# Two float32 blocks on one core: the order on the engines taken from the scheduler's detailed timeline

## The chip, the core and the metric

One core of one Trainium2 chip. The metric is the device time of one execution in microseconds (us). Engines: PE (TensorE), DVE (VectorE), ACT (ScalarE), POOL (GpSimd), SP (SyncE, which issues the loads).

## What is computed

A batch of one, 512 tokens, 1024 features, all in float32. Block 1 is an attention with compressed, selected and windowed keys beside a depthwise convolution of 31 taps, each branch with a merge gate, and then a feed-forward with a convolution of 3 taps. Block 2 has two layers whose norms are modulated by a vector `c`.

```
x = x + (g_a * y_attn + g_b * y_conv) @ w_out            # g_a, g_b: sigmoid of two parts of h @ w_in
x = x + conv_ffn(rms_norm(x, norm2_g), w_up, dw, dw_b, w_down)
return rms_norm(x, final_g)                              # end of block 1
...
mod = silu(c) @ ada_w[layer] + ada_b[layer]              # block 2: shift, scale, gate
h = rms_norm_2(x, norm_w[layer]) * (1.0 + scale) + shift
x = x + gate * mixer(h)                                  # layer 0: dense and latent attention; layer 1: a window with sinks
```

## The kernel before

Features lie on the 128 partitions and the 512 tokens along them, so x is eight tiles of 128x512. A float32 product is made of three matmuls: a weight is split into a high and a low part (`wload`: load L108 by SP, high part L109 by ACT, low part L110 by POOL, for some weights by DVE), the activations likewise, and `mm3` issues low x high (L123), high x low (L124) and high x high (L125). A gemm with 1024 inputs is thus 24 matmuls into one PSUM bank. There are two `pg` and two `ps` banks (the wide gemms go through all four), three `pt` banks for transposes and one `po` bank for attention outputs. A gemm can't begin before the bank that it takes has been read out.

The stages, by the time at which they ran in the profiled execution:
- 0 to 94 us, projections. The first norm's row R1 comes from `Squares` (L209, L216), `rsqrt` (L156 to L170) and a broadcast by PE (L176). The windows for compressed keys are copied by ACT in eight pieces each (L326). The four value gemms of 280 columns (`pg125_516`, `pg128_548`, ...) are read out by ACT (L394). Key stacks are made by ACT (L233, L235) and DVE; the weights of the compression are split at L338.
- 94 to 345 us, attention of block 1, merge gates and the depthwise convolution. Of a half-head (one branch of one head; there are 16) PE makes four score tiles (L501), DVE takes the bias and the maximum (L505), ACT the exponential (L507), DVE a reciprocal (L508), POOL the scaling (L509); PE transposes (L253), ACT and DVE copy it out as two parts (L257, L258), PE multiplies by the values (L263), and L524 adds the compressed branch. DVE's L270 closes a head. The 31 taps over four tiles are 120 DVE instructions at L586 (tap 0 is ACT's). The merge gates are gemms that DVE reads out at L575. Behind the last tap come the layer norm's sums (L601, L602) and L605.
- 345 to 437 us, branch projections and `w_o`. From 437 us the second norm: L170, the chain L156 to L165 on DVE, the broadcast L176 on PE, and R2 copied by DVE at L182.
- 437 to 612 us, up projections of the feed-forward. For every up gemm DVE reads out the bank (L666, it needs R2), ACT starts the convolution (L668), and DVE adds two taps (L670). In between, DVE makes the modulation of block 2: 96 multiply-and-sum instructions at L652 on rows loaded at L651, and 48 small ones at L654.
- 612 to 870 us, down projections; the last one goes by halves of the tokens (`by_halves`: L740 reads a bank out and adds, L722 and L724 make the normed input).
- 870 to 1182 us, layer 0 of block 2 (scores L869, transposes L854, gates as gemms), and 1182 to 1387 us, layer 1.

The order on each engine isn't written by hand. `build` records the instructions in the order of its code; when the `TileContext` closes, its scheduler decides from their dependencies, and from estimates of how long each takes, in which order every engine issues its own. Five places (`with after()`, L247) hold a piece back behind a named instruction. The order is fixed once the program is made: an engine works in that order, and an instruction that waits holds up all that is behind it on its engine.

```
549            with after():
550                conv_start(0)
...
583            for c in range(4):
584                V.scalar_tensor_tensor(conv[c], zs[c][:, t:t + 512], ...)
...
        u = new("p", (128, 514))
        V.tensor_mul(u[:, 2:514], ps, R2)                # L666
```

## Time and profile before

| | |
|---|---|
| median of 3 runs | 1388.19 us (1386.32 to 1389.37) |
| the profiled execution, its span | 1387.6 us |
| busy in the span: PE, DVE, ACT, POOL | 1284.6, 983.8, 690.1, 707.2 us |
[...]

The profiled execution is shown by its span, from the first instruction to the end of the last; it lies 0.6 us under the median. Of PE's 103 us without a matmul some 18 lie in the first 94 us, 24 in the attention of block 1, 21 in the up projections and the norm ahead of them, 9 in the halves around 840 us. In the other stages PE is busy for 95% and more, or the idle time is at the end.

### The profile page before, as it was taken

To read this page: it belongs to the slowest core of one execution; us is meant where nothing else is said; L and a number is where in the kernel's file an instruction comes from. 1 tells how busy PE (TensorE), PEld (TensorE's weight loads), DVE (VectorE), ACT (ScalarE), POOL (GpSimd) and SP (SyncE) were. 2 spreads that over 40 slices of the span, in tenths; PEclk is the share of its full clock that TensorE was granted. 3 is DMA by queue.
4 is the path that set the end of the run, shared out by engine and by line. 5 is a ranking of instruction groups with operands and counts; after the bars stand their busy time and mean duration, and the time that the engine had idled before them with its cause. 6 is when DMAs were issued, how large, how long until landed. Compare 5 with 4: busy or idle time off the path is not lost.

```text
span 1387.6 us, 19249 instructions
## 1 busy us (share of the span) xinstructions
PE 1284.6 (93%) x6337; PEld 1052.3 (76%) x6337; DVE 983.8 (71%) x2117; ACT 690.1 (50%) x1467; POOL 707.2 (51%) x669
## 2 busy tenths in 40 slices
PE   6888889989999998889999997899999989999997
PEld 5777778767877876668888887777777778788886
DVE  7559999984545999972266548967688876666455
ACT  6735467325343323333344434367676745777554
POOL 4248475453643545466555526625444631676642
PEclk9999899999999998999999998999999999999998
DMA  7121101322344777724332320211111120212221
GB/s 222 46 84 56 37 31 56 114 78 82 107 122 129 234 226 228 229 85 137 99 92 78 109 80 26 77 39 35 50 62 39 39 62 28 64 54 62 61 77 61
DMA packets 71971, 124.74 MB, mean 90 GB/s; under 512 B 8256, under 2 KB 17344, under 8 KB 71872
## 3 DMA queue, kind: packets, MB, share of 16 engines
q1 hardware_dynamic: 71872, 123.52, 29.3%
q8 instruction: 50, 0.82, 0.3%
q14 instruction: 49, 0.40, 0.1%
HBM read 121.39 MB, written 2.10 MB: 89 GB/s over the span
## 4 chain that ended last, share of the span: by engine, by line
PE 59%; DVE 28%; ACT 5%; issue 4%; POOL 2%; DMA 2%; SPq 0%; DVEq 0%; ACTq 0%; POOLq 0%
PE pg L123 11%; PE pg L125 10%; PE pg L124 10%; DVE h L586 6%; PE po L263 5%; PE ps L123 4%; PE ps L124 4%; PE ps L125 4%; PE pt L253 3%; DVE p L670 3%; DVE b L652 2%; PE ps L869 2%; DVE z L652 2%; PE ps L1054 2%; PE ps L501 1%
## 5 line engine op out<-in xcount | busy, mean ns | idle before, releaser
L110 POOL TENSOR_TENSOR wl<-wr,wh 128x512 fp32r<-128x512 f32 (+2 forms) x215 | 296.7, 1383 | 319.2 <-ACT wh L109 256.9
L123 PE MATMUL pg<-h,wl 128*128 128x512 f32 x692 | 281.3, 407 | 8.5 <-DVE m L575 5.1
L124 PE MATMUL pg<-h,wh 128*128 128x512 f32 x692 | 277.3, 401 | 0.0
L125 PE MATMUL pg<-h,wh 128*128 128x512 f32 x692 | 276.5, 400 | 0.0
L109 ACT ACTIVATE wh<-wr 128x512 fp32r<-128x512 f32 (+2 forms) x215 | 131.7, 617 | 133.5 <-PE pg L125 74.5
L123 PEld LDWEIGHTS pg<-h,wl 128*128 128x128 f32 x692 | 131.6, 190 | 39.2 <-issue 11.6
L125 PEld LDWEIGHTS pg<-h,wh 128*128 128x128 f32 x692 | 131.6, 190 | 28.3
L124 PEld LDWEIGHTS pg<-h,wh 128*128 128x128 f32 x692 | 131.6, 190 | 27.3 <-issue 0.7
L110 POOL TENSOR_TENSOR m<-t,m 128x512 fp32r<-128x512 f32 (+1 forms) x67 | 93.3, 1392 | 78.7 <-ACT m L109 50.5
L670 DVE SCALAR_TENSOR_TENSOR p<-p,k,p 128x512 f32<-128x512 f32 x88 | 100.4, 1141 | 26.3 <-ACT p L668 25.4
L263 PE MATMUL po<-t,h 128*128 128x512 f32 (+3 forms) x384 | 111.5, 367 | 5.3 <-DVE t L258 2.7
L258 DVE TENSOR_TENSOR t<-pt,t 128x512 fp32r<-128x512 f32 (+1 forms) x160 | 97.3, 629 | 24.9 <-ACT t L257 24.3
L586 DVE SCALAR_TENSOR_TENSOR h<-z,k,h 128x512 f32<-128x512 f32 x120 | 113.4, 988 | 0.1
L257 ACT ACTIVATE t<-pt 128x512 fp32r<-128x512 f32 (+1 forms) x160 | 84.1, 551 | 26.3 <-PE pt L253 25.6
L253 PE MATMUL pt<-k,p 128*128 128x128 f32 x576 | 88.8, 276 | 1.7 <-POOL p L509 0.8
L263 PEld LDWEIGHTS po<-t,h 128*128 128x128 f32 x384 | 67.5, 192 | 27.2 <-ACT t L257 12.0
L253 PEld LDWEIGHTS pt<-k,p 128*128 128x128 f32 x576 | 70.1, 141 | 15.6 <-POOL p L876 3.5
L123 PE MATMUL ps<-h,wl 128*128 128x512 f32 x196 | 78.5, 401 | 1.8 <-ACT h L147 1.6
L124 PE MATMUL ps<-h,wh 128*128 128x512 f32 x196 | 78.0, 398 | 0.3 <-DVE h L148 0.2
L125 PE MATMUL ps<-h,wh 128*128 128x512 f32 x196 | 77.9, 397 | 0.0
L876 POOL TENSOR_SCALAR p<-p,s 128x512 f32<-128x512 f32 x64 | 44.9, 705 | 63.0 <-DVE s L875 62.4
L123 PE MATMUL ps<-h,m 128*128 128x512 f32 (+1 forms) x148 | 59.6, 402 | 15.5 <-DVE p L666 15.4
(367 smaller groups left out, 3003.5 us busy)
## 6 DMA issues: line engine op xcount, KB each, us to landing
b<-ada_t SPq DMA_DIRECT2D x48, 256.0 KB, 3.4
z<-ada_t SPq DMA_DIRECT2D x48, 256.0 KB, 3.4
t<-w_up SPq DMA_DIRECT2D x44, 256.0 KB, 2.9
wr<-w_up SPq DMA_DIRECT2D x44, 256.0 KB, 2.8
wr<-w_g SPq DMA_DIRECT2D x32, 256.0 KB, 2.6
t<-w_dn SPq DMA_DIRECT2D x23, 256.0 KB, 2.7
wr<-w_br SPq DMA_DIRECT2D x16, 256.0 KB, 2.7
wr<-w_gt SPq DMA_DIRECT2D x16, 256.0 KB, 2.7
```

The source lines that it names most:

```text
L109: A.activation(hi[:, :z], raw[:, :z], AF.Copy)
L110: eng.tensor_sub(lo[:, :z], raw[:, :z], f(hi[:, :z]))
L123: PE.matmul(ps, ll, rh, start=start and i == 0, stop=False)
L124: PE.matmul(ps, lh, rl, start=False, stop=False)
L125: PE.matmul(ps, lh, rh, start=False, stop=stop and i == n - 1)
L253: PE.transpose(ps[:, o:o + 128], src, ident)
L257: evac[:] = [A.activation(hi[:, :n], ps[:, :n], AF.Copy)]
L258: evac.append(V.tensor_sub(lo[:, :n], ps[:, :n], f(hi[:, :n])))
L263: PE.matmul(o[:, a:b], v, t[:, pa:pa + b - a], start=start and z == 0, stop=stop and z == 1)
L586: V.scalar_tensor_tensor(conv[c], zs[c][:, t:t + 512], cv("cw", c * 31 + t), conv[c], op0=OP.mult, op1=OP.add)
L652: V.tensor_tensor_reduce(out=raw, in0=raw, in1=CA[z], op0=OP.mult, op1=OP.add, scale=1.0, scalar=0.0, accum_out=acc[:, z:z + 1])
L670: V.scalar_tensor_tensor(t, u[:, i:i + 512], cv("fw", 3 * m + i), t, op0=OP.mult, op1=OP.add)
```

## The change

The context is opened with the scheduler's detailed timeline instead of its simple one. The instructions are the same, 6247 matmuls, 492 loads and all others; their order on the five engines is another.

```diff
-    with tile.TileContext(nc) as tc, ExitStack() as ctx:
+    with tile.TileContext(nc, schedule_with_timeline_sim=True) as tc, ExitStack() as ctx:
```

Three places show what moved. The first is ACT at the key stacks and the value gemms, around 40 us. `p126_541` is what L394 makes of the bank `pg125_516`; `h113` to `h121` are the stacks; `wl151_700`, `wh153_709` are compression weights. Before:

```order
47 L326 ACTIVATE h110_421<-p106_403 64x8x31 x4
48 L233 ACTIVATE h113_461<-p112_459 64x512
49 L235 ACTIVATE h113_461<-p112_459 64x512
50 L233 ACTIVATE h115_467<-p112_459 64x512
51 L235 ACTIVATE h115_467<-p112_459 64x512
52 L233 ACTIVATE h119_500<-p118_498 64x512
53 L235 ACTIVATE h119_500<-p118_498 64x512
54 L233 ACTIVATE h121_506<-p118_498 64x512
55 L235 ACTIVATE h121_506<-p118_498 64x512
56 L394 ACTIVATE p126_541<-pg125_516,s54_269 128x280
57 L338 ACTIVATE wl151_700<-wr150_699 128x2x128
```

And now:

```order
47 L144 ACTIVATE p105_402<-p104_400 128x512
48 L338 ACTIVATE wh153_709<-t152_708 128x2x128
49 L326 ACTIVATE h108_407<-p106_403 64x8x31 x4
50 L326 ACTIVATE h110_421<-p106_403 64x8x31 x4
51 L394 ACTIVATE p126_541<-pg125_516,s54_269 128x280
52 L233 ACTIVATE h113_461<-p112_459 64x512
53 L235 ACTIVATE h113_461<-p112_459 64x512
54 L398 ACTIVATE k124_515<-p126_541 128x24
55 L233 ACTIVATE h115_467<-p112_459 64x512
56 L235 ACTIVATE h115_467<-p112_459 64x512
57 L394 ACTIVATE p129_573<-pg128_548,s54_269 128x280
```

L394 went ahead of the eight stack copies; three of the L338 copies, which followed it, now stand ahead of the L326 pieces.

The second is DVE at the end of the attention of block 1. `h581`, `h460`, `h310` and `h234` are the four tiles of the convolution, `po713_2622` is the output of the last head. Before, the attention is done (its last L270 is number 466 of the engine) and the taps run with the merge gates:

```order
478 L586 SCALAR_TENSOR_TENSOR h581_2229<-z554_2150,k2_107,h581_2229 128x512
479 L586 SCALAR_TENSOR_TENSOR h460_1839<-z427_1722,k2_107,h460_1839 128x512
480 L586 SCALAR_TENSOR_TENSOR h581_2229<-z554_2150,k2_107,h581_2229 128x512
481 L586 SCALAR_TENSOR_TENSOR h234_1071<-z223_1009,k2_107,h234_1071 128x512
482 L575 TENSOR_TENSOR m772_2880<-pg771_2855,r57_284 128x512
483 L586 SCALAR_TENSOR_TENSOR h310_1312<-z283_1233,k2_107,h310_1312 128x512
```

And now the last tap lies behind, and the last head ends with nothing between its own instructions but the gates:

```order
517 L258 TENSOR_TENSOR t719_2640<-pt717_2634,t718_2639 128x512
518 L258 TENSOR_TENSOR t722_2651<-pt720_2647,t721_2650 128x256
519 L575 TENSOR_TENSOR m804_3068<-pg803_3043,r57_284 128x512
520 L508 RECIPROCAL s702_2579<-s702_2579 128x1
521 L258 TENSOR_TENSOR t725_2662<-pt723_2656,t724_2661 128x512
522 L258 TENSOR_TENSOR t728_2673<-pt726_2667,t727_2672 128x512
523 L258 TENSOR_TENSOR t731_2684<-pt729_2680,t730_2683 128x256
524 L145 TENSOR_TENSOR h734_2695<-h236_1075,h733_2694 128x512
525 L145 TENSOR_TENSOR h736_2699<-h360_1492,h735_2698 128x512
526 L145 TENSOR_TENSOR h738_2703<-h487_1920,h737_2702 128x512
527 L270 TENSOR_TENSOR h611_2319<-po713_2622,t732_2691 64x512
```

The taps moved into the attention; the attention's last instructions moved behind them. On PE the merge gates stand correspondingly earlier, mixed with the heads in pieces of one to some twenty matmuls.

The third is DVE at the second norm, from L164 on. `r1056_4288` is R2, `z1105` and the like are loaded modulation rows, `ps1067_4310` is the first up gemm's bank. Before:

```order
635 L164 SCALAR_TENSOR_TENSOR s1054_4274<-s1054_4274 128x4
636 L654 SCALAR_TENSOR_TENSOR k1057_4290<-s1104_4494,k2_107 128x1
637 L165 SCALAR_TENSOR_TENSOR s1053_4273<-s1054_4274,s1053_4273 128x4
638 L652 ISA z1108_4503,s1107_4502<-z1108_4503,z1059_4292 128x512
639 L652 ISA s1107_4502 128x1
640 L182 COPY r1056_4288<-po1055_4283 128x512
641 L652 ISA b1109_4506,s1107_4502<-b1109_4506,z1060_4295 128x512
642 L652 ISA s1107_4502 128x1
643 L666 TENSOR_TENSOR p1068_4335<-ps1067_4310,r1056_4288 128x512
```

And now, from the last instruction of the rsqrt to the first readout:

```order
647 L652 ISA b1155_4710,s1153_4706<-b1155_4710,z1060_4295 128x512
648 L652 ISA s1153_4706 128x1
649 L652 ISA b1158_4718,s1156_4714<-b1158_4718,z1060_4295 128x512
650 L652 ISA s1156_4714 128x1
651 L654 SCALAR_TENSOR_TENSOR k1057_4290<-s1153_4706,k2_107 128x1
652 L652 ISA z1157_4715,s1156_4714<-z1157_4715,z1059_4292 128x512
653 L652 ISA s1156_4714 128x1
654 L654 SCALAR_TENSOR_TENSOR k1057_4290<-s1156_4714,k2_107 128x1
655 L652 ISA z1180_4817,s1179_4816<-z1180_4817,z1059_4292 128x512
656 L652 ISA s1179_4816 128x1
657 L182 COPY r1056_4288<-po1055_4283 128x512
658 L666 TENSOR_TENSOR p1068_4335<-ps1067_4310,r1056_4288 128x512
```

Seven more modulation rows stand ahead of R2, and fewer between the later readouts.

## Rows read from the trace of the kernel before

**Rows 1.** The page, its head and the busy time of the engines (share of the span, number of instructions).

```profile
span 1387.6 us, 19249 instructions
...
PE 1284.6 (93%) x6337; PEld 1052.3 (76%) x6337; DVE 983.8 (71%) x2117; ACT 690.1 (50%) x1467; POOL 707.2 (51%) x669
```

**Rows 2.** Windows by stage: the stretch in us, its length, the busy time of PE, of PE's weight loads, of DVE, ACT and POOL (with the number of instructions), the granted TensorE clock, the DMA share and GB/s.

```profile
0.00:94.00 94.00, 76.27 (x409) 64.90 (x409) 58.80 (x124) 56.87 (x118) 34.77 (x39) 0.96 0.41 127
94.00:244.00 150.00, 135.04 (x699) 110.37 (x699) 141.75 (x357) 87.66 (x222) 98.02 (x106) 0.94 0.14 43
244.00:304.00 60.00, 53.49 (x217) 41.11 (x216) 59.77 (x66) 15.63 (x28) 28.98 (x17) 0.97 0.31 97
304.00:345.00 41.00, 38.83 (x173) 30.11 (x172) 19.16 (x36) 20.38 (x33) 17.25 (x13) 1.00 0.28 83
437.00:612.00 175.00, 153.99 (x622) 121.50 (x622) 167.24 (x355) 55.32 (x89) 89.80 (x61) 0.94 0.68 208
870.00:921.00 51.00, 45.15 (x236) 40.86 (x235) 40.26 (x127) 19.01 (x52) 20.96 (x22) 0.97 0.21 62
```

**Rows 3.** Timeline of PE, 27 to 29 us: start, duration, engine, line, operation, names, and in brackets the idle time before it with what ended it.

```profile
28.03 1.16 PE L176 MATMUL pt<-k,s 128*128 128x128 f32 x8 [2.23 <-DVE s L165]
```

**Rows 4.** Timeline of ACT, 38.9 to 52 us (x8: eight in a row).

```profile
39.14 5.24 ACT L326 ACTIVATE h<-p 64x248 fp32r<-64x248 f32 x8
44.41 0.63 ACT L233 ACTIVATE h<-p 64x512 fp32r<-64x512 f32 x1
...
49.61 0.49 ACT L394 ACTIVATE p<-pg,s 128x280 f32<-128x280 f32 x1
50.00 0.41 ACT L338 ACTIVATE wl<-wr 128x256 fp32r<-128x256 f32 x1
```

**Rows 5.** Timeline of PE, 44.5 to 50.5 us.

```profile
50.15 0.60 PE L123 MATMUL pg<-m,h 128*128 128x280 f32 x1 [5.70 <-ACT p L394]
```

**Rows 6.** Windows around that wait, columns as in Rows 2.

```profile
50.20:55.50 5.30, 5.30 (x25) 5.30 (x26) 2.13 (x5) 2.14 (x8) 1.60 (x2) 0.55 0.27 74
```

**Rows 7.** Groups of DVE by line, 94 to 244 us: names, shapes, number, busy us and mean ns of one, idle time before.

```profile
L586 DVE SCALAR_TENSOR_TENSOR h<-z,k,h 128x512 f32<-128x512 f32 x65 | 59.6, 943 | 0.1
```

**Rows 8.** The same, 244 to 304 us.

```profile
L586 DVE SCALAR_TENSOR_TENSOR h<-z,k,h 128x512 f32<-128x512 f32 x54 | 53.1, 1047 | 0.0
```

**Rows 9.** Groups of POOL by line, 94 to 244 us.

```profile
L509 POOL TENSOR_SCALAR p<-p,s,k 128x128 f32<-128x128 f32 (+1 forms) x64 | 49.5, 779 | 26.6 <-DVE s L508 25.4 <-PE pt L253 1.1
L110 POOL TENSOR_TENSOR wl<-wr,wh 128x512 fp32r<-128x512 f32 x21 | 32.4, 1548 | 17.2 <-ACT wh L109 16.6 <-POOL wl L110 0.4
```

**Rows 10.** All L586 between 160 and 200 us: least, median and greatest duration in ns.

```profile
L586 DVE SCALAR_TENSOR_TENSOR h<-z,k,h x18: 730/742/1779, 159.4 to 198.3; 128x512 f32<-128x512 f32 x18
```

**Rows 11.** Waits of PE, 94 to 304 us: what waited for what, us in total, times, the longest.

```profile
PE ps L501 <- DVE s L505: 6.8, 5, 3.1
```

**Rows 12.** Timeline of PE, 243 to 299 us.

```profile
243.75 0.73 PE L524 MATMUL po<-h,k 32*128 32x512 f32 x2
...
298.40 0.47 PE L123 MATMUL pg<-h,wl 128*128 128x512 f32 x1 [1.46 <-DVE h L575]
```

**Rows 13.** Timeline of DVE, 245 to 305 us.

```profile
245.57 0.69 DVE L270 TENSOR_TENSOR h<-po,t 64x512 f32<-64x512 f32 x1
...
298.18 6.79 DVE L586 SCALAR_TENSOR_TENSOR h<-z,k,h 128x512 f32<-128x512 f32 x7
```

**Rows 14.** Timeline of PE, 304 to 345 us.

```profile
305.72 0.47 PE L123 MATMUL pg<-h,wl 128*128 128x512 f32 x1 [1.46 <-DVE h L575]
```

**Rows 15.** Timeline of DVE, 437 to 460 us.

```profile
445.41 0.69 DVE L182 COPY r<-po 128x512 f32<-128x512 f32 x1 [1.07 <-PE po L176]
...
446.62 0.69 DVE L666 TENSOR_TENSOR p<-ps,r 128x512 f32<-128x512 f32 x1
```

**Rows 16.** Timeline of PE, 461.9 to 462.8 us: where the fifth up gemm begins.

```profile
462.20 0.40 PE L123 MATMUL ps<-h,m 128*128 128x512 f32 x1
462.43 0.39 PE L124 MATMUL ps<-h,m 128*128 128x512 f32 x1
```

**Rows 17.** Timeline of SP's queue, 454 to 455 us: issue of loads.

```profile
454.25 0.38 SPq L651 DMA_DIRECT2D z<-ada_t  x1
```

**Rows 18.** The page, groups of DMA issues: number, KB each, median us from issue to landing.

```profile
z<-ada_t SPq DMA_DIRECT2D x48, 256.0 KB, 3.4
```

**Rows 19.** Groups of DVE by line, 437 to 612 us.

```profile
L652 DVE CUSTOM_DVE_ANT_0 b<-b,z 128x512 f32<-128x512 f32 x48 | 46.3, 964 | 1.2 <-DMA b<-ada_t 1.2
L652 DVE CUSTOM_DVE_ANT_0 z<-z,z 128x512 f32<-128x512 f32 x48 | 39.2, 816 | 0.0
L654 DVE SCALAR_TENSOR_TENSOR k<-s,k 128x1 f32<-128x1 f32 x48 | 19.2, 399 | 0.0
```

**Rows 20.** Timeline of DVE, 604 to 613 us.

```profile
605.91 2.94 DVE L670 SCALAR_TENSOR_TENSOR p<-p,k,p 128x512 f32<-128x512 f32 x2 [1.32 <-ACT p L668]
610.91 0.69 DVE L145 TENSOR_TENSOR h<-p,h 128x512 fp32r<-128x512 f32 x1 [2.07 <-ACT h L144]
611.52 0.68 DVE L666 TENSOR_TENSOR p<-ps,r 128x512 f32<-128x512 f32 x1
```

**Rows 21.** Waits of PE, 812 to 921 us.

```profile
PE pg L123 <- DVE x L740: 8.2, 2, 4.8
PE pg L123 <- DVE p L781: 4.6, 1, 4.6
```

## Prediction

> **What bounds the kernel now.** I read the page first, then the windows by stage, then the waits and timelines of the stages in which PE is not full, and with these in hand the two orders. PE is busy for 93% of the span [rows 1], so a new order can win at most the 103 us in which it has no matmul, and only where something else ends a wait. The windows [rows 2] show where: 17.7 us in the first 94, 21.5 from 94 to 304 us, 21.0 from 437 to 612 us, 5.9 from 870 to 921 us. In the attention (94 to 304 us) and in the up projections (437 to 612 us) DVE is the engine without slack: 141.75 of 150 us, 59.77 of 60 us, 167.24 of 175 us. From 304 us DVE has 19.16 of 41 us and PE is full. A step is therefore priced in the engine that bounds its stage: DVE's work and idle time up to 304 us and in the up projections, PE's waits elsewhere.

> **The start (0 to 94 us): 3.1 us less.** PE stood 5.70 us at the bank that L394 had not read out [rows 5], because L394 lay behind the stack copies: it began at 49.61 us, while the L326 pieces ahead of the stacks ended at 44.4 us [rows 4]. Now L394 follows these pieces. Three L338 copies, 0.41 us each [rows 4], now come earlier: 1.2 us. The first norm's broadcast L176 has moved from the ninth matmul of its gemm to behind all 24, so the wait of 2.23 us ahead of it [rows 3] goes, but R1 comes a little later (15 matmuls at the 0.23 us from one start to the next [rows 16], less 2.2 us: 1.2 us), and the L326 pieces need R1. L394 then begins at 44.4 + 1.2 + 1.2 = 46.8 us and PE goes on 2.8 to 3.1 us earlier; I take 3.1, since part of these copies hides in ACT's waits. The 2.23 us are not added: they are spent in the same wait. [...] Bounds 0 and 8.

> **Attention, gates and convolution (94 to 345 us): 1.7 us given back.** This is the largest move: the merge gates come up to 28 us earlier on PE and the attention's end goes behind them; on DVE the taps mix with the heads.
> - What DVE has to do is equal: up to the last L270 the new order holds the same instructions as the old up to the last tap, but for two small ones on either side. The old reached that point at 304.9 us [rows 13].
> - But what then remains for PE is not. L270 ended 1.8 us behind the last L524 [rows 12, 13], so the new L524 comes at 303.1 us; the rest of one gemm (six matmuls, 1.4 us) and everything from the gemm that used to begin at 298.40 us follow. That took 46.6 us to 345 us, in which waits of 1.46 us [rows 14] fall away with the taps. End: 303.1 + 1.4 + 46.6 - 1.5 = 349.6, 4.6 us later than 345.
> - The taps become cheaper: alone one takes 742 ns, with most above that up to 1779 [rows 10]; the mean was 943 in the attention and 1047 among the gates [rows 7, 8]. All 54 at the lower mean would give 5.6 us; but the POOL splits of the gates' weights (L110), which run beside them, move too; nothing would be the other end. I take the middle, 2.8 us.
> - DVE's own idle time was 8.25 us up to 244 us and 0.2 behind [rows 2]. More taps now fill the heads, none fills the last one. I take no change; ends: all of it gone, or as much again.
> Together -4.6 + 2.8 = 1.8 later, so of the start's 3.1 us some 1.3 remain at 345 us.

> [...] The row shows 943 ns in a stretch in which POOL ran 64 L509 with one input (49.5 us) and 21 L110 with two (32.4 us) [rows 9]. [...]

> **Norm 2 and up projections (437 to 612 us): 3 us less.** The first readout L666 ran at 446.62 us, right behind R2 (L182) and one L652 [rows 15]. Now 13 rows of the modulation stand ahead of R2, 6 before. The last of them is loaded by an issue that ran at 454.25 us [rows 17] and has kept its place in SP's queue; 3.4 us to landing [rows 18], one L652, and R2 comes at 458.5, the first readout at 459.2: 12.6 us later. What covers it is that the first four up gemms have banks of their own: the fifth began at 462.20 us [rows 16]. If R2 came later than that, each us would cost PE one. DVE in these 20.8 us has 13 L652 (0.89 us with its accumulator's 0.08: 12.6), six L654 (0.40: 2.4) [rows 19] and about 1.6 us of chain: 4.2 us idle, about 2 more than before. Against that, the modulation now reaches further: nine of the 96 L652 stand between the 21st and 23rd readout, where DVE idled 1.32 and 2.07 us [rows 20] with none left, and one L670, one L654, one L145 (2.2 us) moved behind the 23rd, whose bank lets the down projections begin (611.52 us). 3.4 + 2.2 - 2 = 3.6; I take 3. Bounds: -4 if DVE loses its waits for loads once more, 10 if the readouts up to the 21st, with 9 L652 fewer ahead, are followed by PE to the end. From there PE is full, so what is won stays.

> **The halves and block 2: 0.5 us less.** Readouts L740 of the second half went ahead of the L724s, and transposes L854 into a gap: PE waited 8.2 and 4.6 us there [rows 21]. I take a quarter, 3 us, since DVE's work stays. In both layers the gates come earlier, up to 25 us, and the last heads lose that cover; at the idle share of 870 to 921 us (5.85 of 51 us [rows 2]) 25 us cost 2.9: I take 2.5. Bounds -8 and 8. Between 345 and 437, 612 and 812 us and at the end nothing of weight moves.

> **Sum.** 1.3 + 3 + 0.5 = 4.8: span 1387.6 - 4.8 = 1382.8, and with the median 0.6 above the profiled span 1383.4 us.

> **The rivals.**
> - *PE waits inside the heads (slower).* With a tap ahead of L505 on DVE, PE's next L501 stands for it, and with it all matmuls behind. Before, PE waited for L505 five times, 6.8 us [rows 11]; there are 64 L505, and taps are now denser. If one more per half-head is late by a tap (0.94 us [rows 7]), 16 x 0.94 = 15 us: 1398.4. It decides from eight such waits on (7.6 us). Against it: PE has gate matmuls in pieces between them.
> - *The taps fill all of the attention (faster).* DVE's 8.5 us of idle time go and the taps get the other half of their discount, 2.8: 1372.1.
> - *Nothing to be told (within 0.2%).* What DVE wins in the up projections goes to its wait for loads ahead of R2, and the rest balances: 4.8 back, 1388.2.
> [...]

> **How the numbers follow.** A measurement of this kernel tells 0.2%, 2.8 us, from no change. The forecast gets 0.40, with a range of its own from 1376 to 1390 (0.24 faster, 0.11 within, 0.05 slower); the waits in the heads 0.24, all slower; the full filler 0.19, all faster; no difference 0.09 (0.02, 0.05, 0.02); the lock 0.08 (0.02, 0.02, 0.04). Faster 0.47, within 0.18, slower 0.35. The range reaches from 1368 (the full filler and some of the start's bound) to 1400 (the heads' waits and a little).

> **What would show it.** Right: PE's wait at L394 under 5 us or begun earlier; the last L524 close to 297 us and PE full from there; L586 under 950 ns; the first L666 near 458 us (459.2 less the 1.3 from before) with no wait of PE at the fifth up gemm; the down projections begun about 4 us earlier. Wrong: waits of L501 for L505 above 14 us, DVE's idle time between 94 and 304 us above 12 us, a wait of several us ahead of the fifth up gemm, or PE under 90% between 921 and 1120 us.

## The result: 1.4% slower, and the profile after

The changed kernel took 1406.3 us (median of 4 runs, 1402.66 to 1408.78) beside 1387.86 us of the kernel before: ratio 1.0137, 95% interval 1.0120 to 1.0154. The profiled execution has a span of 1405.0 us, 17.4 more than [rows 1]. The forecast was 1383.4 us with a range of 1368 to 1400 us, so it missed in sign and in range. What stood nearest was the rival in which PE waits inside the heads (1398.4 us), and its mechanism is only half of what happened.

The page of the changed kernel, to be held against [rows 1]:

```profile
span 1405.0 us, 19242 instructions
...
PE 1293.2 (92%) x6337; PEld 1068.0 (76%) x6337; DVE 999.4 (71%) x2117; ACT 687.6 (49%) x1467; POOL 729.3 (52%) x669
```

The same 6337 matmuls (the page's count for both kernels; the 6247 named with the change is in no row) are busy for 8.6 us longer, and PE stands for 8.8 us longer (1405.0 - 1293.2 = 111.8, before 103.0). So half of the loss is not waiting at all: the granted clock is 0.959 in place of 0.971.

Where it went shows when one asks, for each time of the kernel before, how much later the changed kernel had done the same amount of matmul work (matmuls weighted by their columns, from the two traces). Its delay at PE, in us:

| at (time before) | 90 | 360 | 437 | 640 | 812 | 870 | 1180 | end |
|---|---|---|---|---|---|---|---|---|
| delay | -1.3 | 7.4 | 2.1 | 7.4 | 7.4 | 9.1 | 19.4 | 17.4 |
| change in this stage | -1.3 | 8.7 | -5.3 | 5.3 | 0 | 1.7 | 10.3 | -2.0 |
| forecast | -3.1 | 1.8 | 0 | -3.0 | 0 | -3.0 | 2.5 with the next | |

Where the two orders differ just around a point, a reading is off by a us or so (at 430 us the delay is 3.1, so the two changes beside it would be -4.3 and 4.3). The attention, and layer 0 of block 2 (its last 60 us above all), lose 9 and 10 us. Windows of the changed kernel, cut where it had about the same number of matmuls behind it (columns as in [rows 2]):

```profile
90.50:352.60 262.10, 236.98 (x1094) 187.76 (x1093) 217.66 (x457) 125.55 (x284) 155.87 (x136) 0.92 0.20 61
352.60:440.20 87.60, 87.50 (x377) 70.78 (x378) 48.83 (x58) 37.37 (x63) 49.52 (x36) 1.00 0.38 116
819.50:879.00 59.50, 54.14 (x340) 48.91 (x339) 43.02 (x99) 26.26 (x64) 28.30 (x32) 0.86 0.07 20
1132.00:1202.00 70.00, 60.51 (x357) 54.65 (x358) 43.57 (x95) 28.88 (x63) 18.50 (x14) 0.88 0.15 46
```

and of the kernel before:

```profile
94.00:345.00 251.00, 227.36 (x1086) 181.59 (x1086) 220.69 (x457) 123.67 (x282) 144.25 (x135) 0.96 0.20 63
345.00:437.00 92.00, 90.05 (x386) 72.15 (x384) 43.85 (x54) 37.84 (x63) 47.87 (x35) 0.98 0.37 110
812.00:870.00 58.00, 49.31 (x341) 46.20 (x340) 44.52 (x101) 27.12 (x64) 25.60 (x32) 0.91 0.07 21
1120.00:1182.00 62.00, 56.11 (x358) 51.12 (x356) 43.32 (x95) 29.53 (x62) 17.70 (x14) 0.94 0.16 51
```

In the attention the window is 11.1 us longer, and PE's idle time is 25.1 us in place of 23.6. Eight matmuls more lie in the window (8 x 0.23 [rows 16] = 1.9 us); the other 7.7 us of longer PE time are the clock, 0.92 in place of 0.96. DVE, by which I had priced this stage, is busy for 3 us less than before. Up to its end the attention ran so in the changed kernel (the window, then the last L524 on PE):

```profile
94.00:312.00 218.00, 194.76 (x900) 153.79 (x899) 201.58 (x424) 105.63 (x251) 136.68 (x121) 0.91 0.19 58
```

```profile
303.96 0.73 PE L524 MATMUL po<-h,k 32*128 32x512 f32 x2
```

Why the same idle time costs more clock shows at one place. Before, PE stood 2.82 us once near 201 us and then ran. Now, from the timeline of PE of the changed kernel, 186 to 218 us, the waits among its matmuls:

```profile
194.39 0.79 PE L501 MATMUL ps<-h,h 128*128 128x256 f32 x2 [4.03 <-DVE s L505]
196.52 1.01 PE L501 MATMUL ps<-h,h 128*128 128x384 f32 x2 [0.69 <-DVE s L505]
198.55 1.12 PE L253 MATMUL pt<-k,p 128*128 128x128 f32 x4 [1.02 <-POOL p L509]
206.06 0.55 PE L253 MATMUL pt<-k,p 128*128 128x128 f32 x3 [1.80 <-POOL p L509]
...
214.41 0.65 PE L253 MATMUL pt<-k,p 128*128 128x128 f32 x4 [0.70 <-POOL p L509]
```

The windows there, changed kernel:

```profile
195.00:205.00 10.00, 7.54 (x27) 5.77 (x26) 10.00 (x25) 4.00 (x13) 5.41 (x5) 0.56 0.00 1
205.00:215.00 10.00, 7.96 (x38) 6.21 (x39) 9.94 (x29) 5.78 (x17) 5.89 (x6) 0.83 0.01 2
```

and before, around its single wait:

```profile
200.00:210.00 10.00, 8.95 (x47) 7.78 (x47) 9.55 (x34) 7.79 (x22) 6.30 (x8) 0.83 0.07 26
210.00:220.00 10.00, 10.00 (x62) 8.36 (x62) 9.58 (x30) 7.48 (x21) 7.44 (x9) 1.00 0.28 87
```

In both the granted clock falls to 0.50, before from 201.8 to 205.0 us and now from 193.7 to 203.5 us: with short waits following the long one it is at 0.56 for ten us, from 195 us, and at 0.83 for the ten behind them. The same pattern stands near 108, 137 and 163 us (waits of 2.03 and 1.12, 1.75 and 1.04, 1.63 and 1.02 us), each with a granted clock of 0.50 behind it (110 to 115, 140 to 145, 165 to 170 us). No run changed only how a wait is split, so this is read from the traces and not tested.

In the other engines' rows of this stage, taps and L509 changed places in who pays. All of the attention and gates, changed kernel; the answers to [rows 7 to 9] and [rows 11]:

```profile
L586 DVE SCALAR_TENSOR_TENSOR h<-z,k,h 128x512 f32<-128x512 f32 x120 | 111.7, 943 | 0.9 <-ACT h L421 0.7
...
L509 POOL TENSOR_SCALAR p<-p,s,k 128x128 f32<-128x128 f32 (+1 forms) x64 | 63.7, 997 | 38.8 <-DVE s L508 38.4 <-ACT t L257 0.4
```

```profile
PE ps L501 <- DVE s L505: 13.5, 11, 4.0
PE pt L253 <- POOL p L509: 6.9, 9, 1.8
```

Taps have the lower of their two earlier means, 943 ns. On DVE's busy time this is 113.4 us before and 111.7 now, 1.7 us where I had taken 2.8. L509 went from 779 to 997 ns, which I had not priced. Counted in the two traces, 29 of the 64 L509 ran beside a tap before and 56 in the changed kernel. At 128x128 those took 866 and 983 ns in the mean, the others 447 and 452. So an L509 of this size without a tap beside it costs what it did, and more of them now have one. The lock to which the forecast gives 0.08 is shown by no run.

For the start and the up projections, which the last part comes back to, the rows of the changed kernel are these:

```profile
46.83 0.49 ACT L394 ACTIVATE p<-pg,s 128x280 f32<-128x280 f32 x1
```

```profile
47.38 0.60 PE L123 MATMUL pg<-m,h 128*128 128x280 f32 x1 [4.01 <-ACT p L394]
...
463.34 0.47 PE L123 MATMUL ps<-h,m 128*128 128x512 f32 x1 [1.72 <-DVE p L666]
```

```profile
444.88 0.16 DVE L170 TENSOR_SCALAR s<-ps 128x4 f32<-128x4 f32 x1 [5.53 <-PE ps L217]
...
461.78 0.69 DVE L182 COPY r<-po 128x512 f32<-128x512 f32 x1
462.50 0.69 DVE L666 TENSOR_TENSOR p<-ps,r 128x512 f32<-128x512 f32 x1
```

Before, DVE's wait for the sums was shorter:

```profile
437.68 0.16 DVE L170 TENSOR_SCALAR s<-ps 128x4 f32<-128x4 f32 x1 [1.44 <-PE ps L217]
```

The second loss, changed kernel, PE from 1160 to 1180 us (L176 is the broadcast of the second half's norm):

```profile
1170.13 0.60 PE L176 MATMUL pt<-k,s 128*128 128x128 f32 x4
...
1175.20 0.55 PE L123 MATMUL ps<-m,h 128*128 128x256 f32 x1 [4.46 <-DVE h L724]
```

and the windows behind it:

```profile
1165.00:1170.00 5.00, 5.00 (x31) 5.00 (x31) 1.46 (x9) 0.00 (x0) 0.00 (x0) 0.66 0.00 0
1170.00:1175.00 5.00, 0.74 (x7) 0.55 (x5) 4.22 (x12) 3.96 (x10) 0.00 (x0) 0.81 0.00 0
1175.00:1180.00 5.00, 4.80 (x18) 4.38 (x18) 2.83 (x8) 0.00 (x0) 0.00 (x0) 0.51 0.01 3
```

### The profile page after: what moved, and what is told of

The parts are those of the page before. It is cut to its first block, busy times and chain, and to the rows that moved or that the text cites. A ratio compares the mean times of both kernels' runs of the same rounds, so it can differ in the third digit from the quotient of the medians.

```text
span 1405.0 us, 19242 instructions
## 1 busy us (share of the span) xinstructions
PE 1293.2 (92%) x6337; PEld 1068.0 (76%) x6337; DVE 999.4 (71%) x2117; ACT 687.6 (49%) x1467; POOL 729.3 (52%) x669
## 4 chain that ended last, share of the span: by engine, by line
PE 57%; DVE 28%; issue 7%; POOL 4%; ACT 3%; DMA 1%; SPq 0%; DVEq 0%; POOLq 0%; ACTq 0%
PE pg L123 11%; PE pg L124 10%; PE pg L125 10%; DVE h L586 5%; PE ps L123 5%; PE ps L124 5%; PE ps L125 4%; PE po L263 3%; PE pt L253 3%; DVE p L670 3%; POOL wl L110 2%; DVE z L652 2%; PE ps L869 2%; DVE t L258 2%; DVE b L652 2%
## 5 line engine op out<-in xcount | busy, mean ns | idle before, releaser
L110 POOL TENSOR_TENSOR wl<-wr,wh 128x512 fp32r<-128x512 f32 (+2 forms) x215 | 295.7, 1377 | 274.8 <-ACT wh L109 213.1
L110 POOL TENSOR_TENSOR m<-t,m 128x512 fp32r<-128x512 f32 (+1 forms) x67 | 97.3, 1452 | 82.8 <-ACT m L109 51.4
L586 DVE SCALAR_TENSOR_TENSOR h<-z,k,h 128x512 f32<-128x512 f32 x120 | 111.7, 943 | 0.9 <-ACT h L421 0.7
L253 PE MATMUL pt<-k,p 128*128 128x128 f32 x576 | 97.3, 283 | 8.5 <-POOL p L509 6.9
L670 DVE SCALAR_TENSOR_TENSOR p<-p,k,p 128x512 f32<-128x512 f32 x88 | 95.7, 1090 | 12.3 <-ACT p L668 11.6
L253 PEld LDWEIGHTS pt<-k,p 128*128 128x128 f32 x576 | 73.5, 145 | 27.9 <-POOL p L509 11.8
L509 POOL TENSOR_SCALAR p<-p,s,k 128x128 f32<-128x128 f32 (+1 forms) x64 | 63.7, 997 | 38.8 <-DVE s L508 38.4
L263 PEld LDWEIGHTS po<-t,h 128*128 128x128 f32 x384 | 66.8, 196 | 19.4 <-DVE t L258 8.2
L668 ACT ACTIVATE p<-p,k 128x512 f32<-128x512 f32 x44 | 35.8, 814 | 87.9 <-DVE p L666 87.2
L125 PE MATMUL ps<-h,wh 128*128 128x512 f32 x196 | 77.6, 396 | 0.0
```

Of the source, the lines that this page charges most:

```text
L110: eng.tensor_sub(lo[:, :z], raw[:, :z], f(hi[:, :z]))
L125: PE.matmul(ps, lh, rh, start=False, stop=stop and i == n - 1)
L253: PE.transpose(ps[:, o:o + 128], src, ident)
L263: PE.matmul(o[:, a:b], v, t[:, pa:pa + b - a], start=start and z == 0, stop=stop and z == 1)
L509: G.tensor_scalar(p, p, sm[:, 1:2], GN[:, i, h * 3 + 1 + b:h * 3 + 2 + b], op0=OP.mult, op1=OP.mult)
L586: V.scalar_tensor_tensor(conv[c], zs[c][:, t:t + 512], cv("cw", c * 31 + t), conv[c], op0=OP.mult, op1=OP.add)
```

## The experiments

In most of them only the order differs. It is written out by hand for all five engines, with edges that carry no semaphore, and the context schedules with the simple timeline. In outline:

```diff
         build(ctx, tc, I, out)
+        _pin(nc, tc)
...
+def _pin(nc, tc):
+    for chain in ORDER:            # per engine, the instructions' numbers in the order wanted
+        for prev, i in pairs(chain):
+            tc.add_manual_dep(i, prev, DependencyInfo(NoSync, DATA), reason="order")
```

"New until 90" means: what had begun by 90 us in the changed kernel's trace, in its order, then the rest in the other order. Ratios are to the kernel before, timed beside them; the changed kernel has 1.0137. The diffs of orders below are outlines too.

**One stage at a time.** Each entry is a schedule and the time in that schedule's trace at which it is left.

```diff
+start_only: new 90, old to the end
+attn_old:   new 90, old 345, new to the end
+weo_old:    new 1129, old 1182, new to the end
+mix1:       new 90, old 345, new 440, old 1182, new 1360, old to the end
```

> The issue order of the detailed timeline up to 90 us (everything that had begun by then in its trace), and from there the order of before, written out by hand on all five engines. Theory, each stage stands for itself: the start wins 2.8 to 3.7 us at PE by the two traces, and nothing behind it is changed, so 1387.9 - 3 = 1385 us. Rival, the attention behind it is bound by DVE, which the start does not bring forward: 1387.9 us, no difference, with the lead of 3 us at 90 us gone by 245 us.

Measured: 0.9982 (0.9973 to 0.9991), 1386.3 us. PE is 2.1 us ahead at 90 us and 2.7 at the end, a little less than the theory's 3; the lead is not gone at 245 us.

> The changed kernel with the order of before for what lies between 90 and 345 us (attention of block 1, merge gates, convolution), all else in the new order. Theory: the 11 us that the changed kernel lost there are lost by this order alone, and come back whole: 1406.3 - 11 = 1395 us; PE waits for L505 7 us in 5 waits as before, L509 has its old mean of about 780 ns, the clock of the stretch is 0.94 to 0.95. Rival: what is won there is given back where the next stages are bound by DVE and loads (437 to 620 us), so 1403 to 1406 us.

Measured: 1.0072 (1.0059 to 1.0086), 1399.0 us; PE waits for L505 6.7 us, the clock from 94 us is 0.97. By the ratio 9 us come back, and the time lies between the theory's 1395 and the rival's 1403. Whether the missing 2 us are given back behind, one profile can't tell.

> The changed kernel with the order of before for the end of layer 0 of block 2 and the norm behind it (1120 to 1182 us), all else in the new order. Theory: the 11 us lost there are local (readouts L1011 inside the chain of the rsqrt, the broadcast L176 behind all the matmuls that could have covered it): 1406.3 - 11 = 1395 us, PE over 93% busy from 1120 to 1190 us. Rival: the 4 us that the new order wins in layer 1 are work that these 11 us had done ahead, so only 7 come back: 1399 us.

Measured: 1.0072 (1.0055 to 1.0088), 1398.6 us: about 9 us come back, nearly the rival's 1399, but not for its reason: from 1180 to 1345 us this kernel catches up 4.0 us on the kernel before, as the changed one does, so what layer 1 wins is not the other side of this loss.

> Order of before, with the new order in three places alone: up to 90 us, from 345 to 437 us, and in layer 1 of block 2 (1182 to 1345 us). Theory, stages stand for themselves: -3, -4 and -4 us, so 1387.9 - 11 = 1377 us. Rival, the gains of the later two places are the other side of the losses ahead of them (work that had been done earlier there): only the start's 3 us stay, 1385 us.

Measured: 0.9941 (0.9927 to 0.9955), 1381.7 us: faster than both kernels, by 8 us of the 11 expected. What fell short is the start: in this profile nothing of its lead was left at 140 us. Between 360 and 430 us 4.3 us were won, behind 1180 us 3.8.

A limit of such readings: start_only, attn_old and mix1 have the same order up to 345 us, and their profiles stand at -2.1, -0.7 and +1.3 us there. A stage's figure from one profile is good to about 2 us.

**Is it DVE's order in the heads?** Two kernels in the changed order, with only these rows moved on DVE:

```diff
-L586 taps, L505            (hop1: every L505 from 90 to 312 us)
+L505, L586 taps
-L586 taps, L505 / L508     (hop2: L505 and L508)
+L505 / L508, L586 taps
```

> The changed kernel's order, in which on DVE every L505 of the attention (90 to 312 us) goes ahead of the taps L586 that stood directly ahead of it (68 of its rows move, over 95 taps). Theory: late L505s make PE wait in pairs of waits, and each pair keeps the clock at its lower level, which is where the 11 us of this stage went. PE's waits for L505 then fall from 13.5 to 7 us or less, the clock of the stretch from 90 us to the stage's end goes from 0.92 to 0.95, and the time from 1406.3 to about 1400 us. Rival, DVE is the engine without slack and would only wait for scores instead of doing taps: DVE's idle time grows by what PE wins, and the time stays at 1404 to 1408 us.

Measured: 1.0141 (1.0111 to 1.0172), no gain. Waits of PE, 90 to 353 us, in this kernel:

```profile
PE pt L253 <- POOL p L509: 13.8, 7, 4.6
PE po L263 <- DVE t L258: 3.7, 5, 2.2
PE ps L501 <- DVE s L505: 3.1, 4, 1.8
```

The waits for L505 went from 13.5 to 3.1 us as expected, and those for L509 from 6.9 to 13.8, though an L509 now took 884 ns in place of 997. PE's idle time does not fall (26.4 of 263 us; 25.2 in the changed kernel) and its clock stays at 0.92. The wait had been named after the last thing missing; with that on time, PE stands at the next link of the same chain, L509.

> The same with L505 and the reciprocal L508 ahead of the taps (124 rows over 282 taps), so that POOL's L509 starts earlier and PE's transposes L253 wait less for it (6.9 us in 9 waits in the changed kernel). Theory: the waits for L509 fall under 3 us as well, and the time is 2 to 3 us under the kernel in which L505 alone moves, 1397 to 1398 us. Rival: L508 waits for ACT's exponential, and with it at the front of DVE the taps are held up: 1404 us or more, with DVE's idle time up by several us.

Measured: 1.0231 (1.0203 to 1.0259), 13 us slower still. DVE now idles 12.8 us in front of L508 for ACT's exponential (before this move 2.2), and PE's idle time is 36 us. The rival held. So neither of these two moves on DVE gives the time back. DVE's whole order of before, beside PE's new one, was not run in this stage.

**Is it the taps?** Taps with one input, in the changed order (light) and in the order of before (light_old):

```diff
-                V.scalar_tensor_tensor(conv[c], zs[c][:, t:t + 512], cv("cw", c * 31 + t), conv[c],
-                                       op0=OP.mult, op1=OP.add)
+                V.tensor_scalar(conv[c], zs[c][:, t:t + 512], cv("cw", c * 31 + t), None, op0=OP.mult)
```

> The changed kernel's order, in which the taps L586 only multiply and do not add up what was there (one input read from memory in place of two; the convolution's sum is left out). Theory: POOL's L509 grew from 779 to 997 ns because more two-input taps run beside it; with one input L509 is at 780 ns or less, PE's waits for L509 go from 6.9 us to under 3, and the stage from 90 us to its end is shorter by 5 us or more. Rival: L509 is longer because of what else POOL and the loads do there: it stays over 900 ns.

Measured (two runs): 0.9949 (0.9930 to 0.9967), 1382.0 us. Between 90 and 330 us L509 has 791 ns, PE waits 4.2 us for it, and the stage is 22 us shorter. The stage went as the theory had it, L509 nearly (expected 780 ns or less), PE's waits not quite (expected under 3 us). The taps thus do set L509's time; whether by their inputs or by being shorter isn't told apart, since a tap fell to 642 ns. For the same reason the kernel's time alone tells nothing; that is what the control is for.

> The kernel before with the order of before written out, and taps L586 that only multiply (one input read from memory; the convolution's sum is left out): the control to the same taps in the changed order, which took 1382 us, 24 less than the changed kernel. Theory, the denser taps are what the new order pays for in the attention, by their time on DVE and by what they do to POOL's L509: with light taps the new order loses little there, and this kernel takes 1372 to 1378 us (the changed order with light taps is left with its losses in the other stages, 6 to 9 us). Rival, the order of PE alone costs the 11 us, whatever the taps: this kernel gains as much as the other did, 24 us, and takes 1364 to 1366 us.

Measured: 0.9798 (0.9771 to 0.9826), 1361.7 us. My theory had 1372 to 1378, the rival 1364 to 1366: the rival held in time, by more than it asked. Windows of the attention, light_old and then light:

```profile
94.00:315.00 221.00, 216.47 (x1075) 175.03 (x1074) 184.07 (x453) 124.21 (x279) 125.43 (x134) 0.99 0.22 69
```

```profile
90.00:330.00 240.00, 226.12 (x1095) 181.31 (x1093) 182.14 (x457) 123.85 (x284) 134.47 (x136) 0.97 0.22 66
```

With DVE relieved, PE in the old order stands 4.5 us in this stage, in the new one 13.9. At 345 us they are 12 us apart (with full taps the changed kernel and the one before are 6.4 apart there); the profile of light_old was its fastest run, 5 us under the median, so a part of the 12 may be scatter. The loss is not what a tap costs. It lies in the order, by attn_old in this stage's order; that it is PE's part of it, as the rival has it, is not shown. What is different on PE can be counted: four score tiles (L501) go through two banks, so the matmuls between a tile and the second one behind it are what covers L505, which reads the bank. Summed at 0.233 us for 512 columns (from one start to the next, the median in the changed kernel's trace), the new order has more of it in the mean (3.9 us, before 2.8), because the merge gates are spread over the later heads at about 5 us a tile; but 13 of the 62 pairs have under 1 us (before 7), all among the first 39. Of the 11 waits for L505 (13.5 us) four stand at such pairs, 6.1 us with the 4.03 near 194 us; those near 108 us have 2.5 and 1.5 us of cover. So thin cover goes with about half of these waits. That it is the cause is argued, not shown: a new order with the cover evened out was not tried.

**Does the clock cost what it seems to?** The order of before with 52 matmuls added whose results nobody reads, at the places where PE stands in the attention (before_warm), and the same in the mixed order (mix1_warm):

```diff
+    WARM, calls = {5: 11, 6: 2, 7: 2, 8: 12, 10: 14, 12: 11}, [-1]
     def gemm(src, xs, kt=KT, bank=gemm_bank):
-        w = wsplit(src, kt, 128)
-        ps = bank()
+        w, ps = wsplit(src, kt, 128), bank()
+        calls[0] += 1; [PE.matmul(ps, xs[0][0][:, 0:128], xs[0][0], start=True, stop=True) for _ in range(WARM.get(calls[0], 0))]
```

> The kernel before, its order written out, with 52 added matmuls (128x512, their results are never read) placed on PE ahead of the instructions at which PE stands in the attention of block 1: 11 ahead of the wait of 2.9 us near 98 us, 2 and 2 at 114 and 122 us, 12 near 139 us (3.1 us), 14 near 165 us (3.6 us), 11 near 200 us (2.8 us). At 0.233 us each they are 12.1 us of work for PE. Theory: half of what the changed kernel lost is not waiting but the lower clock behind waits; in the kernel before, the clock falls to half behind these four waits too, 8.4 us lost by the rows (1.7, 1.7, 3.4, 1.7). With PE busy in the waits it does not fall: granted clock from 94 to 245 us from 0.94 to 0.98 or more, and 4 to 8 us less in spite of the added work, 1380 to 1384 us. Rival: the clock has another cause, or DVE, busy for 95% of this stage, is the bound: 1387 to 1389 us; or the added matmuls hold the banks up: 1390 us or more.

Measured: 0.9980 (0.9971 to 0.9990). Windows, before and then before_warm:

```profile
94.00:250.00 156.00, 141.04 (x724) 114.94 (x724) 147.56 (x364) 90.83 (x227) 100.40 (x107) 0.95 0.16 48
```

```profile
94.00:250.00 156.00, 151.05 (x794) 121.24 (x794) 151.75 (x369) 92.61 (x231) 101.17 (x108) 1.00 0.17 56
```

In the same 156 us PE did 70 matmuls more, of which 52 are the added ones; the clock is 1.00 throughout, 0.95 before. Adding work to the waits made the kernel faster, by 0.2%: the low clock there comes from the waits and costs time of its own. The gain is 2.7 us, less than the 4 to 8 expected: the stage was 2.5 us shorter when the last head ended, with DVE busy for 151.75 of the 156 us, and nothing was added behind. So the theory held for the clock, and the time lies at the edge of the rival in which DVE is the bound (1387 to 1389). The order of before written out with nothing added was not run; the nearest controls are w2 (below), which writes out the changed kernel's order but for two broadcasts and takes its time, and the next pair, in which both orders are written out.

> The same 52 matmuls in the mixed order (the new order up to 90 us, from 345 to 437 us and in layer 1 of block 2, the old one elsewhere), which took 0.9941 of the time of before. Theory: the two gains are in different stages and add: 0.990 of the time of before, about 1374 us. Rival as for the kernel before: 0.994.

Measured: 0.9913 (0.9899 to 0.9928), 1377.7 us, the fastest of all: 12 us under the kernel before, 0.28% under mix1, near the theory's 0.990.

**The end of layer 0.** In the changed order, L176 moved ahead over 14 and 9 matmuls (w2), and with it L722 and L724 of the second half interleaved on DVE (w12):

```diff
 PE
-14 (9) matmuls L123 to L125, L176 x4
+L176 x4, 14 (9) matmuls L123 to L125
 DVE (w12)
-L722 x8, L242 x2, L724 x8
+L722 x3, L724 x2, L722, L724, L242 x2, L722, L724, ...
```

> The changed kernel's order, in which on PE the two broadcasts L176 of the norm behind layer 0 go to where the row is ready: 14 matmuls earlier in the first half, 9 in the second (2.4 us each). Theory: DVE waits 3.2 us for the second one, then makes the input for 6.5 us, and PE stands for it; with the broadcast in time PE's wait of 4.5 us falls to about 2, and the clock behind it recovers earlier: 3 to 5 us less, 1402 us. Rival: DVE's own order there (eight L722 before the first L724, readouts inside the rsqrt) sets the wait: under 1.5 us, so 1405 us or more.

> The same, and on DVE in the second half L722 and L724 interleaved as before the change, so that the first input is ready 2.4 us earlier. Theory: both together leave PE under 1 us of wait there and give most of the 8 us that the old order of the whole stage gave: 1399 to 1401 us. Rival: the stage's loss sits ahead of these rows, in the last heads and the readouts L1011: at most 3 us in all, 1403 us or more.

Measured: 1.0137 (1.0101 to 1.0173) and 1.0139 (1.0112 to 1.0166): nothing. The wait of 4.46 us became 3.40 and then 1.75 with one of 0.90 behind it, so the edits did what they should, but in w12 the granted clock was still between 0.50 and 0.83 from 1168 to 1184 us. Both rivals held in time; neither run shows that their reasons are the right ones.

Then PE alone in the new order, with the other four engines in the order of before from 1120 to 1182 us:

```diff
+weo_pe_new: new 1129, old 1182 (PE: the same instructions in the new order), new to the end
```

> The changed kernel with the order of before from 1120 to 1182 us on DVE, ACT, POOL and SP, but the new order on PE (the kernel with all five in the order of before took 1398.6 us, the changed one 1406.3 us). Theory: PE's new order, which has the first half's sums and its broadcast L176 behind the gemms of the second half, leaves nothing to cover the second half's norm, whatever DVE does: 1404 to 1408 us, with a PE wait of 3 us or more ahead of the second half's input. Rival: DVE's new order (the readouts and L724 of the first half ahead of the second half's squares) is what makes the second half late: 1398 to 1401 us.

Measured: 1.0209 (1.0187 to 1.0231), slower than either order whole. PE's waits there:

```profile
1164.32 0.58 PE L123 MATMUL pg<-h,h 128*128 128x256 f32 x1 [7.13 <-DVE x L1011]
1178.28 0.35 PE L123 MATMUL ps<-m,h 128*128 128x256 f32 x1 [1.84 <-DVE h L724]
1183.59 0.79 PE L123 MATMUL pg<-h,wl 128*128 128x512 f32 x1 [4.18 <-DVE h L242]
```

Neither expectation was met (1404 to 1408 and 1398 to 1401 us; measured 1417.4), and the wait ahead of the second half's input was 1.84 us, not 3 or more. What the run does show is that the old order of the other four engines doesn't make PE's new order good. The new order of PE puts the first half's sums and broadcast some 40 matmuls back, among the gemms of the second half. Those are then used up when the second half's norm needs cover; that this is the cause is argued, not shown. How the loss divides between PE and its partners isn't settled: what two orders that don't fit one another cost by themselves, no run shows.

**The up projections.** The order of before from 440 to 612 us in the changed kernel:

```diff
+mod_old: new 440, old 612, new to the end
```

> The changed kernel with the order of before from 440 to 612 us (second norm, up projections, modulation), all else new. By the traces the new order is 4 us ahead at the start of this stage and 4 to 5.6 us behind where it ends. Theory, the modulation's placement costs this (DVE stands 5.5 us for the second norm's sums with nothing ahead of it, and 17 us pass until R2): 1406.3 - 5 = 1401 us, L654's mean back from 547 to about 400 ns. Rival: DVE has the same work to do in either order, and is the bound; what it wins at the norm is not there: 1405 us or more.

Measured: 1.0092 (1.0068 to 1.0115), 1402.1 us: 6 us less by the ratio, as the theory had it. In the profile the stage from 437 to 640 us loses 2.7 us in place of 5.3. L654 in the changed kernel and in mod_old, 437 to 622 us:

```profile
L654 DVE SCALAR_TENSOR_TENSOR k<-s,k 128x1 f32<-128x1 f32 x48 | 26.3, 547 | 0.0
```

```profile
L654 DVE SCALAR_TENSOR_TENSOR k<-s,k 128x1 f32<-128x1 f32 x48 | 18.7, 390 | 0.0
```

Added up, the three stages put back give 1.0137 - 0.0065 - 0.0065 - 0.0045 = 0.9962, and mix1, which takes all three from the old order, has 0.9941. The account closes to within the intervals of the three differences.

## Why the prediction was wrong

- **The start: right in its mechanism.** L394 began at 46.83 us (forecast 46.8), PE's wait was 4.01 us in place of 5.70 [rows 5], and it went on 2.8 us earlier. No run shows the 8 us that I had set as the bound of this step, and of which the range took a part: the wait did not vanish, and the granted clock was 0.50 in the 5.3 us behind it (47.4 to 52.7 us; 0.55 before [rows 6]). At 90 us, by work done, 1.3 us were left of it here and 2.1 in start_only, which has the same order up to there; alone it is worth 0.18%.
- **The attention: the step that failed.** I wrote that a step is priced "in the engine that bounds its stage", DVE here, and took DVE's idle time as unchanged. The last tap did go ahead of the last head and taps did have 943 ns. But the last L524 came at 303.96 us, not at 297, and DVE idled 16.4 us from 94 to 312 us (218.0 less 201.58 busy; up to 304 us it is 13.55), above the 12 us that I had named as the sign of a wrong forecast. DVE's 95% (141.75 of 150 us [rows 2]) was a share that it had in the old order, not a floor of the work. The stage came out 8.7 us later, not 1.8; 7.7 us of it are matmuls at a lower clock. PE waited for a chain that runs through all engines: with L505 moved ahead of the taps (hop1) its waits went from 13.5 to 3.1 us, those for L509 from 6.9 to 13.8, and the time stayed. Of the rival I had the place right (L501 behind L505, 13.5 us in 11 waits), but its mechanism, a tap ahead of L505, fell with hop1. Why the chain is late more often in the new order stays open; thin cover between score tiles goes with 6.1 of the 13.5 us.
- **The clock: a term that was missing.** I kept the clock as it was everywhere. It holds 8.6 of the 17.4 us: 7.7 in the attention, 4.8 in the halves around 840 us, 4.4 at the end of layer 0 (by the PE columns of the windows), less what other stages gained. A clock held up does not give all of it back: before_warm won 2.7 us with DVE busy for 151.75 of 156 us. The changed order with such added matmuls was not run.
- **Up projections: the covering nearly held, the sum had the wrong sign.** R2 came at 461.78 us and the first readout at 462.50 (forecast 458.5 and 459.2; PE entered the stage 2.1 us late). The fifth up gemm waited 1.72 us, and PE's wait of 2.02 us ahead of the broadcast was gone. But DVE stood 5.53 us for the sums with nothing left to do (1.44 before), which the sum didn't have: its bound of -4 was for loads, and the wait for a load was 0.90 us. And L654 grew from 399 to 547 ns, 7.1 us in 48. The mod_old run puts what this order costs at 4 to 6 us.
- **The halves: the wait was right, its worth was not.** PE's waits fell from 8.7 to 5.4 us, the 3 us that I took. They are now nine short ones in place of two long ones of 8.2 us together, and the clock is 0.86 in place of 0.91: busy time 49.31 to 54.14 us. The gain was eaten whole.
- **The end of layer 0: not priced.** I had charged the moved gates to the last heads (2.5 us) and written that nothing of weight moves elsewhere. The norm between the layers was a term of its own: 9 us by weo_old, of which the second half's cover is the likely part. I had also written that PE is busy for 95% and more in the stages that I did not name; from 1120 to 1182 us it was 56.11 of 62 us, at a clock of 0.94, so there was something to lose.
- **Not priced, to the good:** 345 to 437 us, where a wait of 1.63 us and its clock (0.98) went, 4.3 us by work done at 430 us; and layer 1 with the end, 2 us (3.8 in mix1), whose cause no run isolates.

## What to carry to other kernels

Price a new order stage by stage on the engine that must not stop, by the whole chain of instructions that it waits for and not by the link that a wait is named after; a high busy share of another engine isn't a floor (DVE's 95% in the attention wasn't). A wait was worth its length and the lower clock behind it here (7.7 us of the attention's loss are the clock), and by the traces several short ones near each other cost more of it than one or two long ones (in the halves nine of 5.4 us in all stand beside a clock of 0.86, two of 8.2 us beside 0.91): where PE must wait, matmuls that nobody reads can be worth adding (2.7 us in before_warm). And a schedule needn't be taken whole: stages can be cut out of two orders and put together, which here beat both (mix1, 0.9941).
